# A hybrid decoder layer on one core: the first phase's activations turned by DMA transposes instead of TensorE

## The chip, the core and the metric

One core of a Trainium2 chip runs the whole kernel. Its engines are TensorE (PE, with the weight loads shown apart as PEld), VectorE (DVE), ScalarE (ACT), GpSimd (POOL) and SyncE (SP), which here issues nearly all DMAs; each runs its own instructions in order and waits for the others by semaphores. The metric is the device time of one execution in microseconds. Runs of the kernel before: 2116.11, 2118.52 and 2118.77 us, median 2118.52.

## The reference, cut to what matters

One layer over 4096 tokens of width 1024. The first phase computes the modulated norm `h` and everything of the two recurrent mixers; the second phase the sliding-window attention, the gates and the output projection. The change is about the first line only:

```python
h = _rmsnorm(x, g_pre) * (1.0 + scale[:, None]) + shift[:, None]
proj = h @ w_in
aq, ak, av, ag, rkv, rg, gq, gkk, gv, gg = jnp.split(proj, ...)
attn = _sliding_window_attention(aq, ak, av, sinks) * silu(ag)
rwkv = _rwkv7_mixer(h, rr, rk, rv, ...) * silu(rg)
gla = _gla_mixer(h, gq, gkk, gv, ...) * silu(gg)
y = jnp.concatenate([attn, rwkv, gla], axis=-1) @ w_out
return x + gate[:, None] * _rmsnorm(y, g_post)
```

## The kernel before

Tokens are worked through in 16 supertiles of 256 (`NT`). PE contracts over partitions, so `h` must lie with its 1024 features on partitions: `hT` is [128, 2 parts, 8 blocks of features, 256 tokens] in f16, a high and a low part that together carry f32's accuracy; a product takes three f16 matmuls (high by high, high by low, low by high). `hT` has two buffers, and each supertile's is also stored to `hscr` in DRAM for the second phase.

In the first phase each supertile i goes through stages, each a generator in the function `hybrid_kernel`:

- a (`stage_a`): load x into `xt` (one buffer), sum of squares on ACT, inverse root on DVE, scale the rows on DVE in place, 16 transposes of 128x128 in f32 on PE into the PSUM bank "tr" (four at a time, tile `tp`), scale and shift by column on ACT into `hf` (the features are on partitions, so scale and shift are a number per partition), cast to the high part on ACT, subtract for the low part on DVE, store to `hscr` on SP.
- p (`stage_p`): the projections from `hT`: `pv`, `lp`, three of `zz` (k, r, v) and `gqk`, 384 f16 matmuls.
- w (`stage_d`): decays and gates. qa, qb, qc, v, k, q2: RWKV's chunked delta rule. qa writes `RA` (two buffers), `KB` and from them `AT`; `AT`'s 16x16 blocks go to DRAM by eight small DMAs (`adr`) and come back as `AS`; qb runs 15 steps of two DVE operations on `TT`; the result goes out (`tdr`) and comes back (`td`, eight small DMAs); qc combines blocks; q2 walks the four chunks and ends with the transposes `yt`. `RA` of supertile i reuses the buffer that q2 of i-2 read.
- r (`stage_r`): GLA; POOL makes `qb` there, two multiplications of 128x512. POOL also makes `ATm` (a masked copy of `AT`) and copies into `tf` for RWKV. c (`stage_c`): weights for phase two, split in f16 parts in the gaps (tiles `cs`, `ch`, `wscr`, `woscr`).

The order is set in two steps. Streams with ranks (q2 first, then k, qc, qb, qa, v, r, w, a, c, p) are run as generators by `emit`. Then `Order.pin` schedules the recorded instructions anew with a cost for each and pins the outcome as every engine's order: at run time an engine waits for its next instruction even if a later one is ready. In that table of costs an SP transfer is priced by its bytes, whatever its kind, and a POOL operation by its columns, with no term for what DVE does meanwhile. Since helpers record every operation, nearly all instructions bear line 330; they are told apart by the tile names. The second phase (gates `gp`, output products `op`, attention) follows at about 1000 us and isn't touched.

Of the kernel before, what the change touches and what calls it, by code (L numbers as in the profile page):

```python
# [21 lines left out]
P = 128  # L22
D = 1024
T = 4096
NT = 256
NS = T // NT
KD = D // P
HD = 64
# [365 lines left out]
def hybrid_kernel(ctx, tc, x, vecs, rows, adaw, w1, wl, w2, wo, w2aug, a2, gk2, cst, ctr, ctg, abias, out):  # L394
    nc = tc.nc
    model = Model(tc)
    V = Lane(model, nc.vector, *LANES[0])
    S = Lane(model, nc.scalar, *LANES[1])
    G = Lane(model, nc.gpsimd, *LANES[2])
    PE = Lane(model, nc.tensor, *LANES[3], serial=True)  # L400
    SP = Lane(model, nc.sync, *LANES[4])

    def pool_of(at, name, bufs=1, **kw):
        return model.order.pool(at.enter_context(tc.tile_pool(name=name, bufs=bufs, **kw)), bufs)
# [4 lines left out]
    st = pool_of(ctx, "small", 3)  # L409


    ident = cp.tile([P, P], F32, name="ident")
# [34 lines left out]
    hscr = dp.tile([NS, P, 2 * KD * NT], F16, name="hscr")  # L447
# [6 lines left out]
    gs = cp.tile([P, KD], F32, name="gs")  # L454
    sh = cp.tile([P, KD], F32, name="sh")
# [34 lines left out]
    def mq(name):  # L490
        return pst("mq", name)
# [42 lines left out]
    E = [dict() for _ in range(NS)]  # L534
# [11 lines left out]
    def streams(*lst):  # L546
        for rank, name, gen, i in lst:
            live.append([rank, i if i is not None else 0, name, gen(i), (), 0.0, ()])

    def emit():  # L550

        while live:
            live.sort(key=lambda s: s[:2])
            best = None
            for s in live:
                if any(k[1] >= 0 and k not in done for k in s[4]):
                    continue
                t = max([s[5]] + [model.bank(b) for b in s[6]])
                if best is None or t < when:
                    best, when = s, t  # L560
                if t <= PE.clock:
                    break
            assert best is not None, [(s[2], s[1], s[4]) for s in live]
            PE.clock = max(PE.clock, when)
            model.now = PE.clock
            model.lift, model.stage = LIFT.get(best[2], 0), best[2]
            need = next(best[3], done)
            if need is done:
                done.add((best[2], best[1]))
# [71 lines left out]
    with ExitStack() as p1:  # L641

        wk1 = [pool_of(p1, f"work1{n}", 1) for n in "abcd"]
        pp = pool_of(p1, "c1p", 1)
        order = (("hf", "gl", "b1", "zs", "gw", "cgc", "bl", "gk1s", "zl0", "zl1", "zl2", "ch", "cl", "cs"),
                 ("zb0", "zb1", "zb2", "ta", "ep", "em", "b2", "KB"),
                 ("qg", "kg", "egp", "egm", "vg", "c2", "kt", "cd", "em0"))

        def wt(shape, name, bufs=1, dt=F32, tag=None):
            tag = tag or name  # L650
            n = next((n for n, tags in enumerate(order) if tag in tags), 3)
            return wk1[n].tile(shape, dt, tag=tag, name=name, bufs=bufs)
# [40 lines left out]
        nc.scalar.dma_start(CTG, ctg)  # L693
        w2s = pp.tile([HD, 256], F32, name="w2s")
        nc.scalar.dma_start(w2s, w2aug[0:HD, :])
        w0s = pp.tile([HD, 256], F32, name="w0s")
        nc.scalar.dma_start(w0s, w2aug[HD : HD + 1, :].to_broadcast([HD, 256]))
        a2s = pp.tile([P, 256], F32, name="a2s")
        nc.scalar.dma_start(a2s[64:128, :], a2)
# [129 lines left out]
        pow2(hscale, hinv, hs[:, 3:4])  # L829
        V.tensor_scalar(gs, gs, hscale, None, op0=ALU.mult)  # L830
        V.tensor_scalar(sh, sh, hscale, None, op0=ALU.mult)

        for name in ("gv", "gk1", "L"):
            finish_w(name)
# [182 lines left out]
        def stage_a(i):  # L1017

            yield [("a", i - 1), ("p", i - 2)]
            e = E[i]  # L1020
            if i > 0:
                load_x(i)
            xt = e["xt"]
            yield [xt, "tr"]
            xs = [xt[:, a, :] for a in range(2)]
            jx = wt([P, 2, NT], "hf", 2).rearrange("p a n -> p (a n)").bitcast(F16)
            ssx = st.tile([P, 2], F32, tag="ssx", name="ssx")
            for a in range(2):
                S.activation(jx, xs[a], AF.Square, accum_out=ssx[:, a : a + 1])
                yield [ssx]  # L1030
            msx = st.tile([P, 2], F32, tag="msx", name="msx")
            V.tensor_scalar(msx, ssx, 1.0 / D, 1e-6, op0=ALU.mult, op1=ALU.add)
            rsx = st.tile([P, 2], F32, tag="rsx", name="rsx")
            rsqrt(rsx, msx, 2)
            for a in range(2):
                V.tensor_scalar(xs[a], xs[a], rsx[:, a : a + 1], None, op0=ALU.mult)
                yield [xt, "tr"]
            hT = t_hT()
            e["hT"] = hT
            for kp in range(KD // 2):  # L1040

                tag = "tr" if i else ("tr", "y", "sq", "tr")[kp]
                tp = pst(tag, "tp").rearrange("p (a n) -> p a n", a=2)
                for kk in range(2):
                    for a in range(2):
                        k = 2 * kp + kk
                        PE.transpose(tp[:, kk, a * P : (a + 1) * P], xs[a][:, k * P : (k + 1) * P], ident)
                hf = wt([P, 2, NT], "hf", 2)
                for kk in range(2):
                    k = 2 * kp + kk  # L1050
                    S.activation(hf[:, kk, :], tp[:, kk, :], AF.Identity, scale=gs[:, k : k + 1], bias=sh[:, k : k + 1])
                S.activation(hT[:, 0, 2 * kp : 2 * kp + 2, :], hf, AF.Identity)
                V.tensor_sub(hT[:, 1, 2 * kp : 2 * kp + 2, :], hf, hT[:, 0, 2 * kp : 2 * kp + 2, :])
                yield [hf, "tr"] if i else None
            SP.dma_start(hscr[i], hT.rearrange("p a k t -> p (a k t)"))

        def stage_p(i):
# [506 lines left out]
        for i in range(NS):  # L1564
            streams((0, "q2", stage_q2, i), (1, "k", stage_k, i), (2, "qc", stage_qc, i), (3, "qb", stage_qb, i),
                    (4, "qa", stage_qa, i), (5, "v", stage_v, i), (6, "r", stage_r, i), (7, "w", stage_d, i),
                    (8, "a", stage_a, i), (9, "c", stage_c, i), (10, "p", stage_p, i))
        emit()
        model.order.pin()

# [536 lines left out]
```

## Time and profile before

| | |
|---|---|
| profiled execution, its span | 2120.9 us |
| runs (median of 3) | 2118.52 us |
| PE, DVE, ACT, POOL busy, whole span | 93%, 77%, 54%, 10% |
| first `pv` of supertile 0; last `pv` of supertile 15 | 62.8; 955.5 us |
| last `yt` group (end of RWKV's chain) begins | 1113.3 us |
| DMA, mean over the span | 114 GB/s |

The page gives busy times and groups of equal instructions for one profiled execution, whose own time is the span, 2120.9 us; nothing lies around it in that record. It stands 2.4 us over the median of the runs. In rows of groups, "busy" is the union of the group's spans, "mean ns" that of one instruction, and what follows the second bar is idle time of the engine just before such an instruction and what ended it. Matmuls overlap in PE's pipeline, so the step from one to the next is read from the timeline.

### The profile page before, as it was taken

The page shows a single profiled execution, that of the slowest core. Times are in us where ns is not written, and L with a number is a line of the kernel's source. Part 1 is how long each engine was busy: PE and PEld are TensorE (multiplying, and loading weights), DVE is VectorE, ACT ScalarE, POOL GpSimd, SP SyncE. Part 2 cuts the span into 40 slices and gives each one's busy share as a digit, 9 for nine tenths or more (in the row PEclk, how much of TensorE's full clock was granted, in tenths as well). Part 3 has the DMA queues.
Part 4 walks back from the last instruction along what each step waited for, and adds up shares of the span by engine and source line. Part 5 has one row for each costly group of instructions (what it writes and reads, how often), then busy time and mean ns, then how long its engine had stood idle before and what let it go on. Part 6 is the DMA issues. An engine that isn't in the chain of part 4 may idle for free. (4 is left out here: it accounts for less than half of the span.)

```text
span 2120.9 us, 61682 instructions
## 1 busy us (share of the span) xinstructions
PE 1968.3 (93%) x24951; PEld 1538.8 (73%) x24951; DVE 1638.7 (77%) x5261; ACT 1148.0 (54%) x2755; POOL 213.7 (10%) x403
## 2 busy tenths in 40 slices
PE   4799999999999999899876999999999999999996
PEld 3577878778787778777655777777777777777773
DVE  7678778878778688986745888777878877778876
ACT  3776676677766866765314544435444444444442
POOL 2311111421111111111100000000000000000000
PEclk9999999999999999999978999999999999999998
DMA  9332223333232412344115343333343333334342
GB/s 294 126 111 74 77 71 113 97 109 118 77 98 79 132 41 88 114 139 136 58 53 182 128 154 111 131 106 122 111 142 123 123 120 114 112 123 143 107 138 71
DMA packets 187193, 241.98 MB, mean 114 GB/s; under 512 B 52163, under 2 KB 145812, under 8 KB 182678
## 3 DMA queue, kind: packets, MB, share of 16 engines
q1 hardware_dynamic: 185220, 236.76, 35.0%
q8 instruction: 198, 3.24, 0.6%
q10 hardware_dynamic: 1682, 1.21, 0.2%
q14 instruction: 93, 0.76, 0.1%
HBM read 177.08 MB, written 60.82 MB: 112 GB/s over the span
## 5 line engine op out<-in xcount | busy, mean ns | idle before, releaser
L330 PEld LDWEIGHTS <-mtp 128*128 128x128 f16 x1344 | 130.4, 98 | 142.6 <-issue 3.9
L330 PE MATMUL op<-o,mtp 128*128 128x512 f16 x768 | 171.9, 380 | 0.0
L330 ACT ACTIVATE pr<-pr,nm,lsc 128x256 f32<-128x256 f32 (+1 forms) x256 | 149.2, 585 | 36.8 <-DVE nm L330 33.6
L330 PE MATMUL op<-ov,mtp 128*128 128x512 f16 x576 | 145.1, 382 | 2.1 <-ACT mtp L330 2.1
L330 PEld LDWEIGHTS <-hT 128*128 128x128 f16 x1536 | 119.7, 100 | 26.5 <-issue 4.6
L330 DVE TENSOR_TENSOR yv<-op,yv 128x512 f32<-128x512 f32 x112 | 75.1, 681 | 56.6 <-PE op L330 41.4
L330 DVE CUSTOM_DVE_ANT_0 pr<-sc,ab,sinks 128x256 f32<-128x256 f32 (+1 forms) x256 | 107.8, 475 | 8.9 <-PE sc L330 6.3
L330 PE MATMUL pv<-gvh,hT 128*128 128x272 f16 x512 | 98.6, 284 | 7.7 <-DVE kg L330 3.1
L330 ACT ACTIVATE mtp<-yv,oi 128x1024 f16<-128x1024 f32 x32 | 36.6, 1144 | 126.7 <-DVE yv L330 125.2
L330 ACT ACTIVATE ag<-gp,gh 128x512 f32<-128x512 f32 x64 | 43.7, 683 | 106.7 <-PE gp L330 106.7
L330 POOL COPY kT<-kT 128x512 f16<-128x512 f16 x15 | 9.7, 646 | 872.8 <-DVE kT L330 760.5
L330 PE MATMUL lp<-hT,Lh 128*128 128x256 f16 x512 | 93.1, 274 | 0.1
L330 PE MATMUL zz<-hT,rh 128*128 128x256 f16 x512 | 92.0, 279 | 0.0
L330 PE MATMUL gp<-hT,q5h 128*128 128x256 f16 x512 | 91.4, 279 | 0.0
L330 DVE SCALAR_TENSOR_TENSOR ag<-ag,gp 128x512 f32<-128x512 f32 x64 | 43.8, 684 | 61.4 <-ACT ag L330 61.4
L330 PE MATMUL gp<-hT,q3h 128*128 128x256 f16 x512 | 86.9, 275 | 4.1 <-PEq L1965 3.7
L330 PE MATMUL zz<-hT,vh 128*128 128x256 f16 x512 | 89.0, 273 | 1.7 <-DVE zb L330 1.7
L330 PE MATMUL zz<-hT,kh 128*128 128x256 f16 x512 | 90.0, 273 | 0.0
L330 PE MATMUL qp<-hT,q0h 128*128 128x256 f16 x512 | 86.8, 275 | 2.3 <-DVE yv L330 1.5
L330 PE MATMUL gqk<-hT,gqkh 128*128 128x256 f16 x512 | 87.8, 273 | 0.0
L330 PE MATMUL qp<-hT,q1h 128*128 128x256 f16 x512 | 86.2, 273 | 0.0
L330 PE MATMUL gp<-hT,q4h 128*128 128x256 f16 x512 | 85.2, 273 | 0.0
(435 smaller groups left out, 6085.4 us busy)
## 6 DMA issues: line engine op xcount, KB each, us to landing
ov<-woscr SPq DMA_DIRECT2D x96, 512.0 KB, 3.8
xt<-in_x SPq DMA_DIRECT2D x16, 1024.0 KB, 5.4
hscr<-hT SPq DMA_DIRECT2D x16, 1024.0 KB, 5.2
hT<-hscr SPq DMA_DIRECT2D x16, 1024.0 KB, 4.8
out<-yv SPq DMA_DIRECT2D x32, 512.0 KB, 2.9
x<-in_x SPq DMA_DIRECT2D x30, 512.0 KB, 4.2
cs<-in_w SPq DMA_DIRECT2D x112, 128.0 KB, 2.6
v<-vscr SPq DMA_DIRECT2D x128, 64.0 KB, 3.0
```

What stands on the lines that cost most here:

```text
L330: r = f(*args, **kw)
```

## The change

Supertile 0 keeps `stage_a`. For supertiles 1 to 15 a new `stage_at` makes scale, shift and the two f16 parts while tokens are on partitions. Scale and shift are then a row of 1024 numbers, the same in each partition: `spread_rows` makes `gs_row` and `sh_row` once, with four copies of 128x512 on DVE, 16 matmuls against the identity on PE and four ACT copies. Per half of a supertile (128 tokens): ACT squares with a sum, POOL multiplies by `gs_row`, DVE multiplies by the inverse root and adds `sh_row`, ACT casts to f16, DVE subtracts for the low part, and one DMA transpose on SP turns both parts, [128, 2048] in f16 (512 KB), into `hT`. The tile `tok` that holds the parts has one buffer, which the two halves share. The PE transposes `tp` and the tiles `hf` of these 15 supertiles go; `hf` of supertile 0 lies in `tok`.

```diff
-        w0s = pp.tile([HD, 256], F32, name="w0s")
+        w0s = wk1[1].tile([HD, 256], F32, tag="ta", name="w0s")
...
+        gs_row, sh_row = [pp.tile([P, D], F32, name=n) for n in ("gs_row", "sh_row")]
+        def spread_rows():
+            for row, col in ((gs_row, gs), (sh_row, sh)):
+                for g in range(2):
+                    cols = wt([P, 4, P], "spread", 1, tag="gw")
+                    V.tensor_copy(cols, col[:, 4 * g : 4 * g + 4].rearrange("p (k o) -> p k o", o=1).to_broadcast([P, 4, P]))
+                    rp = mq("rowp")
+                    for k in range(4):
+                        PE.matmul(rp[:, k * P : (k + 1) * P], cols[:, k, :], ident, start=True, stop=True)
+                    S.copy(row[:, g * 512 : (g + 1) * 512], rp)
+                    yield ["mq"]
...
+        def stage_at(i):
+            yield [("a", i - 1), ("p", i - 2)]
+            e = E[i]
+            load_x(i)
+            xt = e["xt"]
+            if i == 1:
+                yield from spread_rows()
+            yield [xt]
+            ssx = st.tile([P, 2], F32, tag="ssx", name="ssx")
+            for a in range(2):
+                junk = wt([P, 2, D], "tok", 1, F16)[:, 0, :]
+                S.activation(junk, xt[:, a, :], AF.Square, accum_out=ssx[:, a : a + 1])
+                G.tensor_tensor(xt[:, a, :], xt[:, a, :], gs_row, op=ALU.mult)
+            yield [ssx]
...
+            rsqrt(rsx, msx, 2)
+            yield [xt]
+            hT = t_hT()
+            e["hT"] = hT
+            for a in range(2):
+                V.scalar_tensor_tensor(xt[:, a, :], xt[:, a, :], rsx[:, a : a + 1], sh_row, op0=ALU.mult, op1=ALU.add)
+                tok = wt([P, 2, D], "tok", 1, F16)
+                S.activation(tok[:, 0, :], xt[:, a, :], AF.Identity)
+                yield [tok]
+                V.tensor_sub(tok[:, 1, :], xt[:, a, :], tok[:, 0, :])
+                yield [tok]
+                SP.dma_start_transpose(hT[:, :, :, a * P : (a + 1) * P].rearrange("p b k t -> p (b k) t"),
+                                       tok.rearrange("p b d -> p (b d)"))
+                yield
+            SP.dma_start(hscr[i], hT.rearrange("p a k t -> p (a k t)"))
...
-                    (8, "a", stage_a, i), (9, "c", stage_c, i), (10, "p", stage_p, i))
+                    (8, "a", stage_at if i else stage_a, i), (9, "c", stage_c, i), (10, "p", stage_p, i))
```

The pinned order moves with it. On PE, at the end of supertile 5's projections (`gqk`) and the beginning of supertile 6's (`pv`), there stands before (`tp` are supertile 7's transposes, `X` is a step of qc):

```order
L330 LDWEIGHTS gqkh
L330 MATMUL gqk<-hT,gqkh 128x256
L330 LDWEIGHTS gqkl
L330 MATMUL gqk<-hT,gqkl 128x256
L330 MATMUL tp<-ident,xt 128x128 x8
L330 MATMUL X_6605<-tc_6492,Xs 32x32 x16
L330 LDWEIGHTS hT
L330 MATMUL pv<-gvh,hT 128x272
```

and in the changed kernel at the same place (`gp` is a step of the gate's vector, once in the kernel):

```order
L330 LDWEIGHTS gqkh
L330 MATMUL gqk<-hT,gqkh 128x256
L330 LDWEIGHTS gqkl
L330 MATMUL gqk<-hT,gqkl 128x256
L330 MATMUL gp_6533<-gacc,ones 128x512
L330 LDWEIGHTS hT
L330 MATMUL pv<-gvh,hT 128x272
```

The eight transposes are gone, and `pv` follows `gqk` more closely.

On SP, from supertile 6's `adr` to supertile 8's store `hscr` (`wscr`, `cs` are stage c's weights, `xt` is supertile 9's load), there stands before:

```order
L330 DMA adr<-AT 16x8x16 x8
L330 DMA wscr<-ch 128x256 x4
L330 DMA AS<-adr 64x256 x2
L330 DMA cs<-in_w 128x256 x2
L330 DMA wscr<-ch 128x256 x3
L330 DMA cs<-in_w 128x256
L330 DMA wscr<-ch 128x256
L330 DMA cs<-in_w 128x256
L330 DMA xt<-in_x 128x2x1024
L330 DMA wscr<-ch 128x256 x3
L330 DMA cs<-in_w 128x256
L330 DMA hscr<-hT 128x4096
```

and in the changed kernel:

```order
L330 DMA mscr<-ysb 128x512
L330 DMA_TRANSPOSE hT<-tok 128x16x128 x2
L330 DMA xt<-in_x 128x2x1024
L330 DMA hscr<-hT 128x4096
L330 DMA adr<-AT 16x8x16 x8
L330 DMA AS<-adr 64x256 x2
L330 DMA wscr<-ch 128x256 x3
```

`adr` and `AS` of supertile 6 stood ahead of the load and the store of `hT`; now both transposes, the load and the store of supertile 8 stand ahead of them. In most supertiles the two have changed places in this way.

On POOL, from `tf` of one supertile's qc to the memset of the next `AS`, there stands before (`qb` is GLA's, `zl`, `zs` and `bl` are one-column copies):

```order
L330 TENSOR_TENSOR qb<-qg,bdm 128x512 x2
L330 COPY tf_472<-tc_11207 32x8x32 x4
L330 TENSOR_TENSOR ATm<-AT,tmask 32x256 x4
L330 COPY bl<-bl 128x1
L330 MEMSET AS 128x16
L330 MEMSET vg 128x2
```

and in the changed kernel:

```order
L330 TENSOR_TENSOR qb<-qg,bdm 128x512 x2
L330 COPY tf_474<-tc_8761 32x8x32 x4
L330 COPY bl<-bl 128x1
L330 TENSOR_TENSOR ATm<-AT,tmask 32x256 x4
L330 TENSOR_TENSOR xt<-xt,gs_row 128x1024
L330 COPY zl_9211<-zs 128x2
L330 COPY zs<-zl_8477 128x2
L330 TENSOR_TENSOR xt<-xt,gs_row 128x1024
L330 MEMSET AS 128x16
```

The two multiplications by `gs_row` stand between `ATm` and the memset of `AS`, which DVE's steps on `TT` need.

More of the change, by code (lines that the diff above doesn't have):

```diff
@@ L644, in hybrid_kernel @@
         pp = pool_of(p1, "c1p", 1)
-        order = (("hf", "gl", "b1", "zs", "gw", "cgc", "bl", "gk1s", "zl0", "zl1", "zl2", "ch", "cl", "cs"),
+        order = (("gl", "b1", "zs", "gw", "cgc", "bl", "gk1s", "zl0", "zl1", "zl2", "ch", "cl", "cs"),
                  ("zb0", "zb1", "zb2", "ta", "ep", "em", "b2", "KB"),
@@ L1020, in stage_a @@
             e = E[i]
-            if i > 0:
-                load_x(i)
             xt = e["xt"]
@@ L1025, in stage_a @@
             xs = [xt[:, a, :] for a in range(2)]
-            jx = wt([P, 2, NT], "hf", 2).rearrange("p a n -> p (a n)").bitcast(F16)
+            tok = wt([P, 2, D], "tok", 1, F16)
+            jx, hfs = tok[:, 0, :], tok.bitcast(F32).rearrange("p a (b n) -> p a b n", b=2)
             ssx = st.tile([P, 2], F32, tag="ssx", name="ssx")
@@ L1040, in stage_a @@
             for kp in range(KD // 2):
-                tag = "tr" if i else ("tr", "y", "sq", "tr")[kp]
-                tp = pst(tag, "tp").rearrange("p (a n) -> p a n", a=2)
+                tp = pst(("tr", "y", "sq", "tr")[kp], "tp").rearrange("p (a n) -> p a n", a=2)
                 for kk in range(2):
@@ L1047, in stage_a @@
                         PE.transpose(tp[:, kk, a * P : (a + 1) * P], xs[a][:, k * P : (k + 1) * P], ident)
-                hf = wt([P, 2, NT], "hf", 2)
+                hf = hfs[:, kp % 2]
                 for kk in range(2):
@@ L1053, in stage_a @@
                 V.tensor_sub(hT[:, 1, 2 * kp : 2 * kp + 2, :], hf, hT[:, 0, 2 * kp : 2 * kp + 2, :])
-                yield [hf, "tr"] if i else None
+                yield
[14 more added lines that the diff above has]
+            yield [ssx]
+            msx = st.tile([P, 2], F32, tag="msx", name="msx")
+            V.tensor_scalar(msx, ssx, 1.0 / D, 1e-6, op0=ALU.mult, op1=ALU.add)
+            rsx = st.tile([P, 2], F32, tag="rsx", name="rsx")
+            rsqrt(rsx, msx, 2)
[4 more added lines that the diff above has]
+                V.scalar_tensor_tensor(xt[:, a, :], xt[:, a, :], rsx[:, a : a + 1], sh_row, op0=ALU.mult, op1=ALU.add)
+                tok = wt([P, 2, D], "tok", 1, F16)
+                S.activation(tok[:, 0, :], xt[:, a, :], AF.Identity)
[4 more added lines that the diff above has]
+                                       tok.rearrange("p b d -> p (b d)"))
+                yield
             SP.dma_start(hscr[i], hT.rearrange("p a k t -> p (a k t)"))
```

## Prediction

> **What bounds the kernel now.** I read the page's head first, then the busy times in stretches of 100 us (each engine's busy us, and behind them the granted TensorE clock, the DMA share and GB/s), and then the tile `tp`, which the change takes out of 15 of the 16 supertiles.
>
> ```profile
> span 2120.9 us, 61682 instructions
> 300.00:400.00 100.00, 99.04 (x1523) 80.14 (x1522) 81.58 (x338) 76.17 (x185) 15.76 (x34) 1.00 0.34 105
> 500.00:600.00 100.00, 96.76 (x1578) 79.27 (x1575) 81.78 (x311) 69.67 (x166) 15.48 (x34) 1.00 0.33 103
> 800.00:900.00 100.00, 92.88 (x1308) 75.80 (x1306) 90.64 (x339) 69.01 (x151) 15.12 (x30) 1.00 0.32 91
> ```
>
> In the first phase PE (first busy figure) has 93 to 99 of 100 us, at a granted clock of 1.00; DVE (third) has 82 to 91, ACT (fourth) 69 to 76, POOL (fifth) 15. PE looks like the bound. But two chains meet on it. One is the projections, stage p. The other is RWKV's chain: it begins with the writing of `RA`, goes through `AT`, DMAs to scratch and back, DVE's 15 steps on `TT`, and ends with `q2`, whose last PE work is `yt`. `RA` has two buffers, so supertile i writes it only when q2 of i-2 is done. I looked for that in the timelines, for supertiles 10, 12, 13 and 15:
>
> ```profile
> 812.85 0.63 PE L330 MATMUL yt<-ident,ysb 128*128 128x128 f32 x4
> 837.93 0.68 DVE L330 SCALAR_TENSOR_TENSOR RA<-rn,ep 128x512 f32<-128x512 f32 x1
> 949.36 0.63 PE L330 MATMUL yt<-ident,ysb 128*128 128x128 f32 x4 [0.80 <-DVE ysb L330]
> 1015.28 0.52 PE L330 MATMUL yt<-ident,ysb 128*128 128x128 f32 x3 [0.95 <-DVE ysb L330]
> 1032.35 0.68 DVE L330 SCALAR_TENSOR_TENSOR RA<-rn,ep 128x512 f32<-128x512 f32 x1
> 1113.31 0.55 PE L330 MATMUL yt<-ident,ysb 128*128 128x128 f32 x3 [0.74 <-DVE ysb L330]
> L330 PE MATMUL pv<-gvh,hT x512: 276/279/434, 62.8 to 955.5; 128*128 128x272 f16 x171
> ```
>
> `yt` of 10 is at 812.9, `RA` of 12 at 837.9, `yt` of 12 at 949.4: the loop over two supertiles takes 137 us there. From 13 to 15, with no projections left, it takes 98 us. The last row gives the pace: `pv` runs from 62.8 (supertile 0) to 955.5 (supertile 15), so a supertile takes (955.5 - 62.8)/15 = 59.5 us, two take 119. The loop alone needs 98 of these 119 and `RA` follows `yt` by 17 to 25 us. So PE is full, and the loop has little room: what lengthens it moves the end, and what frees PE helps only as far as the loop lets it.
>
> **The change part by part.** PE first. A row is one group; "busy, mean ns | idle before".
>
> ```profile
> L330 PE MATMUL tp<-ident,xt 128*128 128x128 f32 x256 | 42.1, 286 | 5.8 <-ACT hf L330 4.2 <-DVE xt L330 1.2 <-ACT em L330 0.3
> 406.03 0.60 PE L330 MATMUL tp<-ident,xt 128*128 128x128 f32 x4
> 407.74 0.66 PE L330 MATMUL tp<-ident,xt 128*128 128x128 f32 x4 [1.11 <-ACT hf L330]
> ```
>
> Four transposes take 0.60 us, the last one's own 0.27 included, so they follow each other every (0.60 - 0.27)/3 = 0.11 us; the 286 ns are mostly pipeline. 240 of 256 go: 240 x 0.11 = 26.4 us of PE. The waits that end in `tp` were 5.8 us in all; 5.4 of them go. The 16 matmuls for the two rows come in at 16 x 0.11 = 1.8 us. **PE: -30 us.** No weight or projection matmul changes.
>
> ```profile
> L330 ACT ACTIVATE hf<-tp,sh,gs 128x256 f32<-128x256 f32 x128 | 66.1, 559 | 17.4 <-PE tp L330 15.2 <-DVE wtot L330 1.8
> L330 ACT ACTIVATE hT<-hf 128x512 f16<-128x512 f32 x64 | 40.3, 630 | 0.7
> L330 ACT ACTIVATE hf<-xt 128x1024 f16<-128x1024 f32 x32 | 33.7, 1054 | 5.6 <-DMA xt<-in_x 3.7 <-DVE nwt L330 1.3 <-DVE TT L330 0.4
> L330 DVE TENSOR_TENSOR hT<-hf,hT 128x512 f16<-128x512 f32 x64 | 47.2, 738 | 6.7 <-ACT hT L330 6.6
> L330 DVE TENSOR_SCALAR xt<-xt,rsx 128x1024 f32<-128x1024 f32 x32 | 23.9, 774 | 0.5
> L330 DVE SCALAR_TENSOR_TENSOR yv<-yv,ry,x 128x1024 f32<-128x1024 f32 x32 | 41.1, 1284 | 1.1
> ```
>
> ACT loses 120 x 0.559 + 60 x 0.630 = 105 us and gains 30 casts of 1024 columns at 1.05 (the square's row has that shape) = 32: -73 us. ACT waits for PE already and is 70% busy, so I count this at nothing; it lies beside PE. DVE loses 60 x 0.738 + 30 x 0.774 = 67.5 us. It gains 30 scalar-tensor-tensor of 1024 columns, 1.28 each by the `yv` row, and 30 subtractions to f16 of 1024 columns, twice 0.738: 38.5 + 44.3 = 82.8. With the four small copies that spread the rows, beside supertile 0's projections: **DVE's own work: +15 us.**
>
> POOL gets 30 multiplications of 128x1024. The nearest row is half as wide, and beside it DVE shows something:
>
> ```profile
> L330 POOL TENSOR_TENSOR qb<-qg,bdm 128x512 f32<-128x512 f32 x32 | 36.2, 1151 | 60.9 <-DVE qg L330 49.7 <-DVE yr L330 10.9
> 349.18 2.23 POOL L330 TENSOR_TENSOR qb<-qg,bdm 128x512 f32<-128x512 f32 x2 [7.12 <-DVE qg L330]
> 349.40 2.29 DVE L330 SCALAR_TENSOR_TENSOR rn<-zb,kkh,rn 128x256 f32<-128x256 f32 x2
> L330 DVE SCALAR_TENSOR_TENSOR rn<-zb,kkh,rn x32: 444/480/1269, 100.1 to 1031.5; 128x256 f32<-128x256 f32 x32
> L330 DVE TENSOR_TENSOR AT<-atp,rmask x64: 673/680/692, 117.7 to 1044.5; 128x512 f32<-128x512 f32 x64
> ```
>
> While POOL does its pair in 2.23 us, two DVE operations with both inputs in SBUF take 2.29 us where their median is 0.48 each: 1.33 us lost, 0.6 of POOL's time. `AT`, with one input in PSUM, never stretches (673 to 692). One new multiplication is as long as that pair, 2.2 us, so 30 x 2.23 = 67 us of POOL, and between 0 (DVE always on PSUM inputs) and 67 us of DVE; at the measured 0.6, **40 us**. The new subtractions and `RA`, `rn`, `TT` on the loop are such operations. [...]
>
> So DVE has 15 + 40 = 55 us more. The longest waits of PE between 100 and 1000 us (total, times, longest) end with it:
>
> ```profile
> PE pv L330 <- DVE kg L330: 3.1, 2, 1.6
> PE X L330 <- DVE Xs L330: 3.0, 3, 1.6
> PE ot L330 <- DVE bon L330: 2.5, 1, 2.5
> ```
>
> Yet DVE idles 9 to 18% of the stretches above. Bounds on the path: 0 and 55; the loop is made of DVE steps for about half, so I take half: **+27 us.**
>
> The transposes on SP. No DMA transpose is in the trace. Below, the size in KB and then the us to landing; and SP's time for an issue (min/median/max, ns).
>
> ```profile
> out<-yv SPq DMA_DIRECT2D x32, 512.0 KB, 2.9
> ov<-woscr SPq DMA_DIRECT2D x96, 512.0 KB, 3.8
> xt<-in_x SPq DMA_DIRECT2D x16, 1024.0 KB, 5.4
> hscr<-hT SPq DMA_DIRECT2D x16, 1024.0 KB, 5.2
> adr<-AT SPq DMA_DIRECT2D x128, 8.0 KB, 1.5
> L330 SPq DMA_DIRECT2D adr<-AT x128: 302/428/1542, 121.8 to 1047.8; - x128
> DMA to landing us min/median/max: 1.4/1.5/5.1
> ```
>
> One transpose moves 512 KB. Lower end: a plain 512 KB transfer, 2.9 us. Upper end: `adr` moves 8 KB in small pieces and holds SP 0.428 us; 64 of these make 512 KB, 27.4 us. I take 6 us, near the plain row, as it is one instruction of full size. [...]
>
> Whether activations come too late for `pv` is not the question at 6 us: transposes of i are issued while i-1 is projected. What counts is who stands behind them. SP is in order, and where before `adr` of the RWKV chain stood ahead of the load of x and the store `hscr`, it now stands, in most supertiles, behind two transposes, the load, and the store, which waits for both transposes to land. `AS`, POOL's `ATm` and DVE's `TT` steps wait behind `adr`. Price: 8 KB behind the 2 MB lands after up to 5.1 us instead of 1.5 (+3.6), and the store's wait adds up to a transpose, 0 to 6 us, if `adr` was ready by then. I take 3.6 + 2 = 5.6 us a supertile; the loop spans two supertiles, so 2.8 us each, x 14 = 39 us at most, 0 at least (when `AT` is late anyway). Half: **+18 us** (with what the new POOL work holds up in POOL's queue).
>
> Sum: -30 + 27 + 18 = **+15 us**. The profiled span, 2120.9, stands 2.4 us over the median of the runs, 2118.5; on the median that is 2133.5.
>
> **The rivals.**
>
> A, my forecast: the loop takes PE's place as the bound; 2133. For it: 98 us unloaded in a 119 us frame, all new costs lying on its engines. Its own range is 2123 to 2165 (all bounds at the high end: -30 + 55 + 39 = +64, over 2180, is unlikely together).
>
> B, the other side: PE stays the bound and the loop hides DVE's and SP's extra in its 21 us. Then -30 us less a few us of DVE: 2093, range 2088 to 2114. For it: PE's 99% of 300 to 400, the 73 us that ACT gets back, and the PSUM bank "tr", now left to stage w alone. Decides: the loop lengthening by less than about 4 us per two supertiles. Against: DVE's 90.6% in 800 to 900.
>
> C, transposes far dearer, 20 us or more: two of them hold SP for 55 of 59.5 us, and the loop's 20 small issues at 0.43 us (8.6 us) alone make it 63.6; SP bounds the phase, and activations reach `pv` late. At least (63.6 - 59.5) x 15 = 62 us, with SP's other issues some 100: 2220 or more.
>
> D, both sides cancel: 2114 to 2123.
>
> **How the numbers follow.** A 0.44, B 0.31, C 0.12, D 0.13. Predicted is A's 2133. 0.2% of 2118.5 is 4.2 us, about what a measurement can tell from no change. Faster (B) 0.31, same (D) 0.13, slower (A and C) 0.56. The range 2092 to 2185 leaves out C and the lowest part of B.
>
> **What would show it.** Right, if `tp` counts 16 and PE's busy share in 300 to 900 falls below 93 to 97%; if 128x1024 on POOL takes 2.2 us and `rn`, `RA` and the new `hT`/`tok` subtraction show many at over twice their median; if `adr` lands in 4 to 5 us instead of 1.5; if `yt` to `yt` over two supertiles exceeds 119 us. Wrong, if the pace of `pv` falls under 58.5 us (B), or if SP waits over 15 us for a landing of `hT` (C). The working fails first where half of DVE's extra is put on the path: no row gives that share.

## The result, and the profile after

The changed kernel takes 2201.66 us (median of 4 runs, 2199.86 to 2203.09) where the kernel before, run beside it, took 2118.64: a ratio of 1.0388, 95% interval 1.0371 to 1.0405, or 82 us more. I had forecast 2133 and a range up to 2185.

The head of the page:

```profile
span 2199.0 us, 61208 instructions
```

By tiles, the pace row of `pv`, the row of `yt` and that of the transposes that are left (min/median/max of one in ns, then first and last start in us); the last row is `yt` in the kernel before:

```profile
L330 PE MATMUL pv<-gvh,hT x512: 276/279/434, 64.1 to 1032.6; 128*128 128x272 f16 x171
L330 PE MATMUL yt<-ident,ysb x64: 272/273/472, 238.1 to 1183.8; 128*128 128x128 f32 x64
L330 PE MATMUL tp<-ident,xt x16: 421/421/475, 33.3 to 63.5; 128*128 128x128 f32 x16
```

```profile
L330 PE MATMUL yt<-ident,ysb x64: 272/273/447, 211.7 to 1113.7; 128*128 128x128 f32 x64
```

The 240 transposes are gone, and yet a supertile takes (1032.6 - 64.1)/15 = 64.6 us instead of 59.5. RWKV's last `yt` stands 70 us later than before (1183.8 against 1113.7), and the span has grown by 78: nearly all of the loss is in the first phase. PE shows it. The busy times of one long stretch, 100 to 1000 us, first of before and then of the changed kernel (PE, PEld, DVE, ACT, POOL, then granted clock, DMA share, GB/s):

```profile
100.00:1000.00 900.00, 863.75 (x13417) 700.85 (x13416) 718.37 (x2588) 620.45 (x1457) 164.31 (x320) 1.00 0.32 98
```

```profile
100.00:1000.00 900.00, 818.54 (x12328) 648.47 (x12327) 706.78 (x2361) 522.77 (x1209) 228.10 (x332) 0.97 0.38 100
```

PE is idle for 81 of 900 us where it was idle for 36; DVE and ACT are idler too, POOL alone has more to do. No engine is full: what was saved on PE, and more, has become waiting. PE's granted clock is also lower, 0.97 instead of 1.00; over 900 us that is 27 us of PE's time at most, as an estimate. The waits of PE in the same stretch (total, times, longest) do not name one culprit:

```profile
PE yt L330 <- DVE ysb L330: 7.6, 5, 2.9
PE rp L330 <- DVE Ss L330: 6.6, 3, 4.5
PE gap L330 <- DVE qb L330: 6.2, 2, 3.1
PE bp L330 <- ACT UV L330: 6.1, 3, 3.2
PE sp L330 <- ACT UV L330: 5.7, 7, 2.1
PE kvp L330 <- DVE Gst L330: 5.3, 1, 5.3
```

Before, the largest total there was 3.1 us. These are waits of RWKV's and GLA's small steps on DVE and ACT, a few us each, spread over many tiles.

The added operations cost about what I had put down for them:

```profile
L330 POOL TENSOR_TENSOR xt<-xt,gs_row 128x1024 f32<-128x1024 f32 x30 | 71.6, 2398 | 66.7 <-ACT tok L330 43.6 <-DVE qb L330 9.0 <-DMA adr<-AT 7.7
L330 DVE SCALAR_TENSOR_TENSOR xt<-xt,rsx,sh_row 128x1024 f32<-128x1024 f32 x30 | 38.9, 1306 | 0.7
L330 DVE TENSOR_TENSOR tok<-xt,tok 128x1024 f16<-128x1024 f32 x30 | 38.3, 1276 | 16.7 <-ACT tok L330 16.7
```

and on SP the issue of a transpose (ns), its landing (us), and `adr` (us to landing):

```profile
L330 SPq DMA_TRANSPOSE hT<-tok x30: 1317/1981/3353, 93.9 to 975.0; - x30
DMA to landing us min/median/max: 4.3/5.3/6.6
adr<-AT SPq DMA_DIRECT2D x128, 8.0 KB, 2.0
```

A multiplication on POOL takes 2.4 us (2.2 taken), the scalar-tensor-tensor 1.31 (1.28), the subtraction 1.28 (1.48), a transpose holds SP for 1.98 us and lands after 5.3 (6 taken), and `adr` lands after 2.0 us (1.5 before), not after 5.1. The single operations were priced nearly right and the whole came out 69 us too low. The experiments had to find what lies between.

### The profile page after: what moved, and what is told of

It reads as the page before. It is cut to its first block, busy times and chain, and to the rows that moved or that the text cites. A ratio compares the mean times of both kernels' runs of the same rounds, so it can differ in the third digit from the quotient of the medians.

```text
span 2199.0 us, 61208 instructions
## 1 busy us (share of the span) xinstructions
PE 1978.9 (90%) x24743; PEld 1533.0 (70%) x24743; DVE 1695.8 (77%) x5235; ACT 1092.2 (50%) x2607; POOL 288.0 (13%) x433
## 5 line engine op out<-in xcount | busy, mean ns | idle before, releaser
L330 PE MATMUL zz<-hT,kh 128*128 128x256 f16 x512 | 95.2, 283 | 1.0 <-ACT vg L330 1.0
L330 DVE SCALAR_TENSOR_TENSOR ag<-ag,gp 128x512 f32<-128x512 f32 x64 | 43.8, 684 | 64.6 <-ACT ag L330 64.6
L330 ACT ACTIVATE tok<-xt 128x1024 f16<-128x1024 f32 x62 | 65.4, 1055 | 53.2 <-DMA hT<-tok 18.0
L330 PE MATMUL sc<-kT,q 128*128 128x256 f16 (+1 forms) x512 | 72.7, 276 | 18.3 <-DVE m L330 14.5
```

Source lines behind the costliest of these rows:

```text
L330: r = f(*args, **kw)
```

## The experiments

Ratios are to runs of the kernel before on the same chip; 1% is 21.2 us.

**First, the costs one by one, in the changed kernel's own order.** The planner pins each engine's order by the sizes it sees, so an experiment that shrinks an operation would also get another order. These kernels tell the planner the old size; each engine's order is then that of the changed kernel, row for row, and only the durations differ.

`e1_thin`, POOL's multiplications on 8 of 1024 columns:

```diff
-                G.tensor_tensor(xt[:, a, :], xt[:, a, :], gs_row, op=ALU.mult)
+                G.tensor_tensor(xt[:, a, 0:8], xt[:, a, 0:8], gs_row[:, 0:8], op=ALU.mult)
```

> The two POOL multiplications of a supertile shrink from 1024 to 8 columns (so most of the scale is left out); every engine keeps exactly the order of the changed kernel, since the planner is still told 1024. Three theories share the 83 us that the changed kernel is longer. P, POOL's multiplications (DVE's operations stretch by 33 us more than before, and what stands behind 2.35 us pieces on POOL comes late): here at least 40 us come back, 2160 us or less. S, SP's queue (transposes that hold SP for 2 us, land after 5.3 us and stand with the store of hT ahead of adr): at most 12 us come back, 2190 or more. O, the order that was pinned with the wrong prices, and DVE's own added work of 15 us: at most 20 us, 2180 or more.

Measured: 2171.87 us, ratio 1.0286 (1.0259 to 1.0313). That is 1.02%, 22 us, back (some 15 to 28 by the two intervals). Between all the theories: POOL costs more than S allowed, about O's upper end, and half of what P asked for. How it costs shows in one place of the changed kernel, a timeline of all engines:

```profile
476.58 0.29 DVE L330 TENSOR_TENSOR Ss<-sp,Sst 128x128 f32<-128x128 f32 x1 [0.46 <-PE sp L330]
476.66 2.35 POOL L330 TENSOR_TENSOR xt<-xt,gs_row 128x1024 f32<-128x1024 f32 x1
...
476.90 2.25 DVE L330 TENSOR_TENSOR Sst<-Ss,cd 128x128 f32<-128x128 f32 x1
...
479.21 0.27 PE L330 MATMUL rp<-Sst,RA 64*64 64x64 f32 x1 [0.82 <-DVE Sst L330]
```

`Sst` is RWKV's state, a step of q2, and takes 0.29 us on the median of 64. Here it starts 0.24 us after a multiplication on POOL, ends 0.14 us after it, and PE's `rp`, the next step of q2, waits for it. With thin multiplications the longest `Sst` takes 1.14 us instead of 2.25.

`e2_plain`, the transposes as plain transfers of the same bytes:

```diff
-                SP.dma_start_transpose(hT[:, :, :, a * P : (a + 1) * P].rearrange("p b k t -> p (b k) t"),
-                                       tok.rearrange("p b d -> p (b d)"))
+                SP.dma_start(hT[:, :, :, a * P : (a + 1) * P].rearrange("p b k t -> p (b k) t"),
+                             tok.rearrange("p b (k t) -> p (b k) t", t=P))
```

> The DMA transposes become plain transfers of the same 512 KB from tok to hT, at the same places (the activations are then not turned, so the values are others); all orders are those of the changed kernel. S: issue and landing fall from 2.0 and 5.3 us to some 0.1 and 3 us, and at least 30 us come back: 2172 or less. P: under 10 us come back, 2192 or more. O: under 10 us, 2192 or more.

Measured: 2195.53 us, ratio 1.0385 (1.0360 to 1.0410): nothing back. SP's rows for these transfers, issue (ns) and landing:

```profile
L330 SPq DMA_DIRECT2D hT<-tok x30: 606/648/659, 93.3 to 966.9; - x30
DMA to landing us min/median/max: 4.2/4.6/6.7
```

So 1.3 us less of SP and 0.7 us less to landing per transfer are worth nothing here: S falls in this order. The run leaves `adr` behind the same transfers, so it does not try the whole of my term for SP. The timelines do: from the end of `AT` to the last of its eight `adr` issues it is 6.6 us on the mean of supertiles 1 to 14, and 4.5 before, so `adr` is 2.1 us later on SP and 0.5 us later from issue to landing: 2.6 us, where I had taken 5.6.

`e3_thin_plain`, both edits:

> Both edits at once, 8-column multiplications and plain transfers, in the changed kernel's order (scale mostly left out, activations not turned). P and S together: what is left is -30 us of PE against +15 of DVE in the loop, so 2110 to 2140. O: the order itself costs most, so 2170 or more remain. If the gains of the two single edits add up to this run's gain, they are separate costs; if this run gains less than the larger of them plus 5 us, they are one wait seen from two sides.

Measured: 2165.69 us, ratio 1.0242 (1.0221 to 1.0262), 31 us back; 51 us remain. The 9 us beyond `e1_thin` are the most that the transposes' own time can be given, and the two intervals overlap.

`e5_free` makes DVE's new operations thin as well, in the same way, and lets ACT's cast write both parts:

```diff
+                V.scalar_tensor_tensor(xt[:, a, 0:8], xt[:, a, 0:8], rsx[:, a : a + 1], sh_row[:, 0:8], op0=ALU.mult, op1=ALU.add)
+                S.activation(tok, xt[:, a : a + 1, :].to_broadcast([P, 2, D]), AF.Identity)
+                V.tensor_sub(tok[:, 1, 0:8], xt[:, a, 0:8], tok[:, 0, 0:8])
```

> All the new work made nearly free in the changed kernel's order: multiplication, scalar-tensor-tensor and subtraction on 8 columns, plain transfers (ACT's cast writes both parts, so that the transfer has data; the activations are neither scaled, shifted nor turned). The planner is told the full sizes, so each engine's order is that of the changed kernel. The run with thin multiplications and plain transfers stood 51 us over before, so neither POOL nor SP holds most of the loss. W, DVE's own new work (30 times 1.28 and 1.2 us, 75 us, all behind or ahead of the RWKV loop's steps): at least 50 us come back against that run, at or below before, 2115 or less. O, the order that was pinned: under 25 us come back, 2140 or more, though PE and DVE have 30 and 67 us less to do than in before.

Measured: 2164.98 us, ratio 1.0243 (1.0223 to 1.0263), no less than `e3_thin_plain`. Its stretch from 100 to 1000 us:

```profile
100.00:1000.00 900.00, 829.87 (x12680) 660.31 (x12679) 646.91 (x2461) 563.06 (x1249) 159.08 (x335) 0.98 0.37 104
```

DVE has 647 us of work instead of before's 718, POOL 159 instead of 164, PE has the transposes less, and the kernel is still 51 us longer than before, with PE idle for 70 us. W falls. What is left of the change in this kernel is the order of the instructions and what hangs on it, the waits for buffers and PE's lower clock among them; ACT's casts and 30 plain transfers of 512 KB are still there too.

**Second, other orders for the same work.** First a look whether any new order of a kernel costs this much. `e7_before_sp050` and `e8_before_tiling05` are the kernel before with one constant of the planner changed (`st.occ = 0.50`, `TILING_WAIT = 0.5`):

> A control: the kernel before, whose planner is told 0.50 instead of 0.47 us for an SP issue; nothing else, so only the pinned order differs (some thousands of rows). O: the order of before is a good draw, and a new one costs 1% or more, 2140 or more. W and P: under 0.5%, 2108 to 2129.

> A second control: the kernel before with the planner's wait for PE's tiling at 0.5 instead of 0.6 us; only the pinned order differs. O: 1% or more slower, 2140 or more. W and P: under 0.5%, 2108 to 2129.

Measured: 2119.89 us, ratio 1.0019 (1.0005 to 1.0032), and 2121.99 us, ratio 1.0032 (1.0021 to 1.0043). Thousands of rows change places and the time moves by 0.2 and 0.3%, both times upwards: before's order is not a rare stroke of luck.

For the changed kernel it is otherwise, though the edits that redraw its order are larger ones; the two small constants were not tried on it. `e4_price` tells the planner what the trace shows:

```diff
-            st.occ = 0.47
+            st.occ = 2.0 if name == "dma_start_transpose" else 0.47
...
-                st.occ = 0.42 + 1.5e-3 * n if n <= 512 else 1.85e-3 * n
+                st.occ = 0.42 + 1.5e-3 * n if n <= 512 else 2.3e-3 * n
```

> The changed kernel with the planner told what the trace shows: a DMA transpose holds SP for 2.0 us and lands after 5.4, a POOL multiplication of 1024 columns takes 2.36 us. The computation is the whole one, only the pinned order differs. O: at least 25 us come back, 2176 or less. P and S: the costs stay where they are, within 12 us of 2202.

Measured: 2186.4 us, ratio 1.0341 (1.0314 to 1.0368), 10 us back. `e6_lag` sets the activations back (`LAG = {"l": 150, "a": 500}`):

> The changed kernel with the activations' steps set back by 500 ranks in the planner (about a quarter of a supertile), so that the RWKV loop's steps go ahead of them on DVE, POOL and SP; the computation is the whole one. hT is ready 30 to 40 us before pv needs it in the changed kernel. If the loss is that activations stand ahead of KB, adr and AS (legs that are 8 to 14 us and 5 us later than before): at least 25 us come back, 2177 or less. If it is the amount of work (W, P): within 12 us of 2202. If the planner's order is fragile in general (O): either sign, by 10 us or more.

Measured: 2210.86 us, ratio 1.0441 (1.0418 to 1.0464), 11 us worse. The edit did not do what it was meant to: in its trace both transposes and both multiplications of supertile i + 2 still stand ahead of `adr` and `AT` of supertile i, for i from 2 to 13, as in the changed kernel. It shows another order, and not what the activations' place is worth.

In the timelines of these kernels something else stood out. `D`, the block that qc starts from, is done, and its first product `Xp` on PE comes much later. In the changed kernel, supertile 2, DVE's row and PE's row:

```profile
309.40 0.44 DVE L330 STREAM_TRANSPOSE D<-td 128x256 f32<-128x256 f32 x1
```

```profile
327.97 0.75 PE L330 MATMUL Xp<-D,ATm 32*32 32x32 f32 x64
```

18 us lie between, in which PE works mostly on `pv`, `lp` and `zz` of supertile 4. Over supertiles 1 to 14 (start of the first `Xp` less start of `D`, whose own 0.4 us is included, from the timelines) the mean is 9.2 us, 3.9 before, and over supertiles 3 to 14 `RA` follows the first `yt` of two supertiles earlier by 3 us on the mean, 18 before. My guess, theory T: the planner's first step, which walks the streams along a clock of PE's work, lost the transposes from its clock, so the streams were recorded in another sequence, and `Xp` takes its turn in the PSUM bank "mq" too late. Three kernels, all with the whole computation. `e9_clock` gives the clock its 4.4 us a supertile back, in two halves:

```diff
+                PE.clock += 2.2
                 yield [tok]
                 SP.dma_start_transpose(hT[:, :, :, a * P : (a + 1) * P].rearrange("p b k t -> p (b k) t"),
```

> The changed kernel, whole computation, with one number of the planner restored: the first step of the planning walks the streams along a clock of PE's work, and counted 0.27 us for each of the 16 transposes; with them gone its clock runs 4.4 us a supertile short. This kernel adds the 4.4 us to that clock and nothing to the program. T, a new theory: because of that clock the streams are recorded in another order, the RWKV chain's steps take the PSUM bank mq in another sequence, and Xp, the first product of qc, stands behind the next supertile's projections on PE (from D to Xp 9.2 us on the mean in the changed kernel, 3.9 before). By T: D to Xp under 5 us, yt to RA back above 12 us, and at least 40 us come back, 2160 or less. If the loss is in the changed kernel's work and dependencies themselves: within 12 us of 2202.

Measured: 2161.0 us, ratio 1.0188 (1.0165 to 1.0211); 42 us back, `D` to `Xp` 2.0 us, `yt` to `RA` 16.8.

`e10_price_clock` has this and the prices of `e4_price`:

> As the run with the planner's clock restored, and with the prices of the transposes (2.0 and 5.4 us) and of POOL's multiplication (2.36 us) put right as well. T: 5 to 20 us less than with the clock alone, if prices and clock are separate errors. Work and dependencies: within 20 us of 2202.

Measured: 2198.65 us, ratio 1.0391 (1.0367 to 1.0415). `D` to `Xp` is 1.9 us and `yt` to `RA` 17.6, as T wants, and nothing comes back. Against `e9_clock`, only prices in the planner differ, and 43 us lie between the two. `e11_p_after_qa` holds the stream of projections back by a condition:

```diff
-            yield [("a", i), ("p", i - 1), ("r", i - 2)]
+            yield [("a", i), ("p", i - 1), ("r", i - 2), ("qa", i - 1)]
```

> The changed kernel, whole computation, with another remedy for the same thing: the stream of projections p of supertile i is not recorded before qa of i-1 is through, so that qc cannot be recorded behind them. T: as with the clock restored, at least 40 us come back, 2160 or less, D to Xp under 5 us. If the clock restores something else than the place of qc: this one stays within 20 us of 2202.

Measured: 2144.01 us, ratio 1.0116 (1.0097 to 1.0135). **58 of the 82 us come back with the computation whole and every added operation in place.** `D` to `Xp` is 2.3 us. PE is idle for 72 us of the stretch instead of 81:

```profile
100.00:1000.00 900.00, 827.72 (x12654) 659.71 (x12655) 746.66 (x2530) 554.53 (x1282) 231.64 (x339) 0.97 0.42 111
```

and the last `yt` begins 50 us earlier, the last `pv` 33 us:

```profile
L330 PE MATMUL yt<-ident,ysb x64: 272/273/476, 217.7 to 1133.8; 128*128 128x128 f32 x64
L330 PE MATMUL pv<-gvh,hT x512: 276/279/434, 63.6 to 999.3; 128*128 128x272 f16 x171
```

The activations' place is not what was mended: both transposes and both multiplications of supertile i + 2 still stand ahead of `adr` and `AT` of i here in all but one of the supertiles 2 to 13.

The same rule in the kernel before, as a control (`e13_before_p_after_qa`):

> The control for the better order: the kernel before with the same extra condition on the stream of projections (p of i not recorded before qa of i-1), whole computation. T (the changed kernel's record order had gone wrong, that of before had not): no gain here, 2110 to 2150. If the condition is simply a better rule for any kernel: 2100 or less, and then the changed kernel's own work costs 44 us or more.

Measured: 2131.66 us, ratio 1.0084 (1.0059 to 1.0109). In the kernel before, the rule costs 18 us: it is no better in itself, and mends something in the changed kernel's order.

Then T's own place, without touching a rule of the planner. `e17_qc_on_tr` gives qc's tiles the bank "tr", which the change had left nearly empty:

```diff
-            yield [D0, ATm, "mq"]
-            Xp = mq("Xp")
+            yield [D0, ATm, "tr"]
+            Xp = pst("tr", "Xp")
```

(and `Xq`, the second `Xp` and `X2` likewise).

> The changed kernel, whole computation, with the tiles of qc (Xp, Xq, X2) in the PSUM bank tr, which the PE transposes had used before and which the change left to stage w alone, instead of the bank mq, where they took turns with yt, kp, vp, np, atp, kvp and gap. T, the place is the turn in the bank mq: D to Xp under 5 us, and at least 40 us come back, 2160 or less. If the gap from D to Xp only goes along with the loss and isn't its cause: D to Xp falls and under 20 us come back, 2182 or more.

Measured: 2189.29 us, ratio 1.0347 (1.0325 to 1.0369). `D` to `Xp` falls to 3.0 us, `yt` to `RA` is 16.5, and 9 us come back. The last three supertiles still have the loop tight there (`RA` 2 to 5 us after `yt`); `e10_price_clock` has neither mark and is as slow as the changed kernel. Together they speak against T: the late `Xp` and the tight loop are marks of one bad order, and do not carry the loss.

`e18_qc_on_tr_pqa` joins this with the rule of `e11_p_after_qa`:

> The same with p recorded after qa as well, whole computation. If both remedies cure one thing: within 8 us of the better of the two. If they are separate: 10 us or more below it, 2134 or less. To beat the kernel before it would have to give back the 15 us of POOL's multiplications, which no order takes away, so 2118 or less is not expected by any of the theories.

Measured: 2172.09 us, ratio 1.0267 (1.0242 to 1.0292): 32 us worse than the rule alone, which neither expectation allowed. `e16_pqa_st1_pe`, with the rule of `e11_p_after_qa`, leaves supertile 1, too, to PE (`stage_at if i > 1 else stage_a`), since the changed kernel's `yt` of supertile 1 was already 43 us late (311.1 against 267.9):

> The run with p recorded after qa, but supertile 1 keeps the activations by PE as supertile 0 does; supertiles 2 to 15 by DMA. Whole computation. If the start (supertile 1's multiplications, cast and transposes beside the splitting of the weights and the spreading of the rows) still costs what the traces say, 11 us by the end of supertile 1: 5 to 12 us back, 2132 to 2139. If the loss is spread over all supertiles: within 4 us of 2144.

Measured: 2153.45 us, ratio 1.0194 (1.0169 to 1.0220), 17 us worse than `e11_p_after_qa`, where 5 to 12 better was expected; the order is another one again. `yt` of supertile 1 comes at 281.5 us, 278.9 in `e11_p_after_qa`: what lateness is left at the start there did not go with supertile 1's new work.

**Third, the costs again, in the best order.** With the rule of `e11_p_after_qa`, and its order kept row for row, `e14_pqa_thin` has the edit of `e1_thin`:

> The run with p recorded after qa (2144), its order kept exactly, POOL's multiplications on 8 columns instead of 1024 (most of the scale is left out). P, POOL and the port: 15 to 30 us back, 2114 to 2129. If POOL's cost came from the bad order only: under 8 us, 2136 or more.

("The port" is short there for what DVE's operations last longer while POOL multiplies, as `Sst` above with 2.25 us instead of 0.29; what makes them last longer no run shows.)

Measured: 2126.06 us, ratio 1.0043 (1.0027 to 1.0059). POOL's multiplications cost 1.16 - 0.43 = 0.73%, 15 us, in a good order.

and `e15_pqa_free` all those of `e5_free`:

> The same order again with all the new work nearly free: multiplication, scalar-tensor-tensor and subtraction on 8 columns, plain transfers (activations neither scaled, shifted nor turned). By the sum of my prediction PE's -30 us should now stand alone, and half of it should arrive as in the run with one transpose of four: 2095 to 2108. If the order still holds a good part: 2115 or more.

Measured: 2116.23 us, ratio 1.0015 (1.0001 to 1.0029). DVE's new operations and the transposes together cost 0.28%, 6 us. What remains is a kernel with nearly all the new work gone and 240 transposes fewer on PE, and it is not faster than before. `e5_free` has the same instructions in the changed kernel's order and stands at 1.0243: between the two lies nothing but the order, and it is 2.28%, 48 us. The stretch of `e15_pqa_free`:

```profile
100.00:1000.00 900.00, 844.71 (x13161) 676.48 (x13161) 670.91 (x2582) 585.18 (x1307) 161.92 (x345) 0.98 0.40 112
```

PE is idle for 55 us where it was 36 before. And the relief alone, in an order near before's (not the same row for row), with one transpose of four (`e12_quarter_tp`; the planner is told four):

```diff
-                for kk in range(2):
-                    for a in range(2):
+                for kk in range(1 if i else 2):
+                    for a in range(1 if i else 2):
...
+                    S.activation(hf[:, kk, :], tp[:, 0:1, 0:P].to_broadcast([P, 2, P]) if i else tp[:, kk, :], AF.Identity, scale=gs[:, k : k + 1], bias=sh[:, k : k + 1])
```

> What is PE's relief worth in the order of before? The kernel before with one PE transpose of four in supertiles 1 to 15 (the planner is told four; ACT reads the one in place of the four, so the activations are others): PE has 180 x 0.11 = 20 us less to do, nothing is added. If PE is the bound of before: 17 to 22 us less, 2096 to 2102. If PE and the RWKV loop share it as I had forecast (the loop with 17 to 25 us of room): 5 to 15 us less. If the loop alone: 0 to 5.

Measured: 2109.43 us, ratio 0.9952 (0.9936 to 0.9969). Of 20 us taken from PE, 10 arrive (7 to 14 by the interval). Its order is drawn anew too, and two new orders of before cost 4 and 7 us (`e7_before_sp050`, `e8_before_tiling05`), so the half is rough.

```profile
100.00:1000.00 900.00, 856.29 (x13277) 685.98 (x13270) 722.10 (x2599) 620.83 (x1458) 163.15 (x320) 0.99 0.32 99
```

No kernel that makes the activations by DMA, with the whole computation, came below the kernel before.

## Why the prediction was wrong

The side was right, the size was not. Step by step, with what the runs put in place of each term:

| step of the prediction | forecast | shown |
|---|---|---|
| PE: 240 transposes go | -30 | no gain, +3 (0 to 6), in the best order, whose own cost is in it (`e15_pqa_free`); -10 of 20 near before's (`e12_quarter_tp`) |
| DVE's own work and what its operations last longer beside POOL's, half of 55 | +27 | POOL 15 (`e14_pqa_thin`) to 22 (`e1_thin`); DVE with the transposes 6 (`e14_pqa_thin` less `e15_pqa_free`) |
| SP's queue and `adr` | +18 | the transposes' own time 0 (`e2_plain`), at most 9 (`e3_thin_plain`); `adr` 2.6 us later a supertile, not 5.6 |
| the order that the planner draws for the changed steps | no term | +58 (`e11_p_after_qa`) |
| sum | +15 | 3 + 6 + 15 + 58 = +82 |

**The step that failed is the sum, "-30 + 27 + 18 = +15 us", because it had no term for the order, which cost 58 us against the best order tried.** I followed instructions that changed places at three spots and priced the waits there, and took the rest of the order as given. It wasn't. Nine kernels with the activations by DMA and the whole computation (one of them with supertile 1 on PE), that differ in their order and in two cases in a PSUM bank, lie between 1.0116 and 1.0441 of before, a spread of 69 us. Four orders of the kernel before lie between 1 and 1.0084. That the order costs this much is shown by two pairs with the same work: 58 us between the changed kernel and `e11_p_after_qa`, 48 between `e5_free` and `e15_pqa_free`. **Which place in the order costs it stays open.** The late `Xp` and the tight loop do not carry it: `e9_clock`, `e10_price_clock` and `e17_qc_on_tr` all have `yt` to `RA` at 16 us or more on the mean of supertiles 3 to 14 and differ by 43 us. Nor does the place of the activations, which `e11_p_after_qa` kept. Of the 70 us by which the last `yt` is late, 43 are there at supertile 1, where `e11_p_after_qa` is 11 late; but that kernel is 60 late at supertile 11 and 20 at the end, so the early loss alone doesn't decide. The traces only show what a bad order looks like: many small waits on PE, none of them long, and a lower clock beside them.

**The clock is a rival that no run separates.** In the first 1200 us the records hold 72 us at a granted clock of 0.50 before, 130 in the changed kernel, 140 in `e10_price_clock`, 89 in `e11_p_after_qa` and 68 in `e15_pqa_free`. PE does about half as much there: in the changed kernel's first 1100 us the products of `pv` follow each other every 227 ns on the median at 0.50 (from 439.1 to 442.4 us, for one) and every 116 ns at 1.00. So the 58 us more in the changed kernel are worth up to 29 us, an estimate from these numbers. Whether the clock adds this to the cost of the order's waits, or only shows time in which PE had to wait anyway, is not shown.

**-30 us counted in full** is the second failure. I had written that PE "looks like the bound" and that two chains meet on it, and then subtracted PE's saving as if it were alone. A busy share of 93 to 99% did not mean that time taken from PE is time gained: about half arrived in `e12_quarter_tp`, none in `e15_pqa_free`, where the cost of the new order may hide a part. The room that I gave the loop, 17 to 25 us from `yt` to `RA`, was read from two pairs; over supertiles 2 to 15 of before it runs from 1.5 to 29.8.

**DVE beside POOL.** The size was near. Take what DVE's operations last over the median of their kind, for all that last more than 1.12 times that median, from 100 to 1000 us: 28 us before, 57 in the changed kernel, 29 more where I had 40, and 29 in all in `e1_thin`. So the thin multiplications take the stretch away, and with it 15 to 22 us of the time, about the half of 40 that I had taken. The victims were not those I named. In the changed kernel `rn` (at most 0.49 us) and `RA` (at most 0.69) never stretched; `Sst` did, and so did operations with a single tensor as input (the last row is `gw` in `e1_thin`):

```profile
L330 DVE SCALAR_TENSOR_TENSOR RA<-rn,ep x16: 672/683/691, 121.4 to 1078.5; 128x512 f32<-128x512 f32 x16
L330 DVE TENSOR_TENSOR Sst<-Ss,cd x64: 248/286/2254, 205.5 to 1177.5; 128x128 f32<-128x128 f32 x64
L330 DVE TENSOR_SCALAR gw<-gw x16: 407/428/2359, 114.4 to 1053.7; 128x512 f32<-128x512 f32 x16
L330 DVE COPY em<-em x16: 146/170/2203, 120.6 to 1063.3; 128x2 f32<-128x2 f32 x16
```

```profile
L330 DVE TENSOR_SCALAR gw<-gw x16: 408/427/666, 109.8 to 1017.5; 128x512 f32<-128x512 f32 x16
```

The longest operations of the changed kernel's `Sst`, `gw` and `em`, 2.20 to 2.36 us, last about as long as one multiplication on POOL (2.36 on the median).

**SP.** The guess of 6 us for a transpose was near (5.3), and that activations would not come late was right. `adr` landed after 2.0 us and not after 5.1, all in all it came 2.6 us later and not 5.6, and where the queue was relieved nothing came back. (Half of 39 is 19.5; the 18 of the prediction is a slip that changes nothing.)

**The rivals.** A, the loop in PE's place: the changed kernel fits it (`RA` 3 us after `yt`, two supertiles from `yt` to `yt` in 126 us instead of 120), but orders with 16 us of room were as slow, so the tight loop alone is not the cause. Of A's other signs, `tp` counts 16, PE's busy share from 300 to 900 us fell from 96 to 92%, and POOL's multiplication takes 2.36 us; the stretched `rn` and `RA` and the slow `adr` did not come. B, PE still the bound, is refuted by the result; even with the new work nearly free (`e15_pqa_free`) its -30 us did not come. C, dear transposes, is refuted by their row (5.3 us to landing, 1.98 us of SP). D, that both sides cancel, was not seen with the work in place.

**The range** ended at 2185 because it added up bounds of named costs. For a kernel whose every row is placed anew by a planner it should have held the planner's own spread as well.

## What to carry to other kernels

Where a planner pins each engine's order, a change is two changes: its work and a new order; price the first, and before believing a measurement draw several orders of the changed kernel and of the old one (other prices in the planner, or one more condition), since here that spread was 69 us and the loss in the best order 25. To price a part of the work, shrink it while the planner is told the old size, so that every row stays in place. And where an engine is 95% busy but two chains meet on it, don't count its saving in full: here about half of it arrived, or none.

## What the runs showed of the hardware

A DMA transpose of 512 KB from SBUF to SBUF in f16 (128x2048) held SP for 1.98 us on the median, and landed after 5.3 us; a plain transfer in its place 0.65 and 4.6 us. POOL's 128x1024 multiplication in f32 took 2.36 us on the median and held up, for nearly its whole length, some of DVE's operations: `gw` over 128x512 took 0.43 us on the median and 2.36 at the longest (with multiplications of 128x8 the longest was 0.67), a copy of 128x2 0.17 and 2.20 (0.17 at the longest before). And more idle time on PE went along with a lower clock: in the stretch from 100 to 1000 us PE is idle for 81 us at a granted clock of 0.97 in the changed kernel, and for 36 us at 1.00 before. In the first 1200 us the records of both kernels show the clock at 1.00 or 0.50, at 0.50 in intervals that last 3.41 us or a multiple of it; those that begin between 100 and 1100 us add up to 75 us in the changed kernel, 41 before, and 48 in `e15_pqa_free`.
